# A hybrid diffusion step on one core: two groups of small products per chunk in the recurrence, and another order at the entry

## The chip, the core and the metric

The kernel runs on one core of a Trainium2 chip. The core has five engines with a queue of instructions each: TensorE (PE: matrix products into PSUM, which has eight banks per partition), VectorE (DVE), ScalarE (ACT), GpSimd (POOL) and SyncE (SP, which here only issues transfers). An engine runs its queue in order; semaphores make it wait for the others. The metric is the device time of one execution in microseconds.

## The reference

One layer of a diffusion backbone over 1024 latent and 128 context tokens of width 1024: half a SwiGLU block, a token mixer, half a SwiGLU block, a last norm. Shift, scale and gate of each norm come from a conditioning vector through a linear map. The mixer runs latent attention beside a gated linear recurrence (HGRN2), forward and backward, eight heads of 64 × 64:

```python
b = jnp.cumsum(logf.reshape(B, n, CHUNK, H, DK), axis=2)
A = jnp.einsum('bntshk,bnthk,bnshk->bnhts', decay, qc, kc)
o_intra = jnp.einsum('bnhts,bnshv->bnthv', A, vc)
dS = jnp.einsum('bnshk,bnshv->bnhkv', kc * jnp.exp(g[:, :, None] - b), vc)
def step(S, inp):
    gj, dSj = inp
    return jnp.exp(gj)[..., None] * S + dSj, S
o_inter = jnp.einsum('bnthk,bnhkv->bnthv', qc * jnp.exp(b), S_prev)
```

All is float32; the large products are made of three products of rounded parts (high × high, low × high, high × low).

## The kernel before

A builder takes the instructions as the program records them, makes every dependence into a semaphore wait, and sets each engine's order by priorities and assumed costs of its own; `keep_in_program_order` pins some of them. So the order on an engine is not always that of the code.

**Entry** (`consts`, `start`). Three small transfers (the conditioning vectors cc, the vectors vec, an identity) and then the large ones are issued on SyncE: for each of eight tiles of the model width two transfers of the conditioning weights (wada) and one of the tokens (x), with two weight tiles (raw) near the front. TensorE sums the conditioning for tile k (`sums`, L159), turns it (`vectors`, L175), ScalarE and VectorE scale and split the tokens (`split`, L532 and L533), and TensorE adds the tile's part to seven running products (`unit`, names ps, bh, bl, wh, wl). `consts` also makes the recurrence's lower bounds from two exponentials on ScalarE (L305, L306).

**Recurrence** (`hgrn`). Eight heads of three chunks of 384 tokens make 24 chunks. A chunk is worked by a pair of generators. `scan_pre` makes decayed keys and queries (Kb, Qb, KE, QP) on ScalarE, VectorE and GpSimd. `scan_lev` has steps, each ending at a `yield`:

- the first products: keys by queries inside blocks of 32, one half of the partitions per direction, into two PSUM banks (lv), from which VectorE's masked copy (COPY_PREDICATED, L1093) takes the parts within blocks of 8 into A1 and A2;
- levels 8, 16, 32 and 64: products of KE's halves (kr) by QP into one more lv bank (L1086), a copy out, and the scaling of KE and QP for the next level (L1123);
- the transposed keys (kt, L1138), and then the state products dS (L1148).

After a head's third chunk `scan_out` runs the state chain S (L1158) and the output products po (L1168, L1171). The lv tiles share three banks in turn. `group` runs such steps one after the other, so that their small products stand together on TensorE; between groups `slots` lays projection products (mm: 128 × 384, in halves of 12) that belong to other parts of the mixer. A chunk has three groups, and two chunks are in flight: the first products with level 32 of the chunk before; level 8 with that chunk's level 64 and transposes; level 16 with its dS.

Of the kernel before, what the change touches and what calls it, by code (L numbers as in the profile page):

```python
# [9 lines left out]
F32 = mybir.dt.float32  # L10
# [3 lines left out]
AF = mybir.ActivationFunctionType  # L14
# [5 lines left out]
P = 128  # L20
# [7 lines left out]
NCH = T // CW  # L28
# [5 lines left out]
H = 8  # L34
# [59 lines left out]
class Trunk:  # L94
# [27 lines left out]
    def start(self):  # L122
        nc, a, pp, fp = self.nc, self.a, self.pp, self.fp
        pin = self.tc.keep_in_program_order
# [72 lines left out]

        var = {}
# [27 lines left out]
        self.lnexp()  # L226
# [4 lines left out]
        ps = {u: self.bank(t, "ps", cols[u[1]]) for u, t in zip(units, homes)}  # L231
        vectors(0, sums(0))
        for k in range(KT):
            last = k == KT - 1
# [6 lines left out]
            if k and not last:  # L241
                row = sums(k + 1)
# [37 lines left out]
    def consts(self):  # L280
        nc, cp, a = self.nc, self.cp, self.a
        self.cc = cp.tile([P, KT, 2], F32, name="cc")
        nc.sync.dma_start(self.cc, a["cc"])
# [13 lines left out]
        self.hg = self.vec[:, 109:110]  # L297
        g0, g1 = self.vec[:, 110:118], self.vec[:, 118:126]
# [6 lines left out]
        nc.scalar.activation(e0, e0, AF.Exp)  # L305
        nc.scalar.activation(e1, e1, AF.Exp)  # L306
# [559 lines left out]
    def hgrn(self):  # L866
# [145 lines left out]
    def scan_pre(self, d, b):  # L1012
# [42 lines left out]
        nc.gpsimd.tensor_tensor(e8(qp), e8(Qb), bc(TQ, 8), ALU.mult)  # L1055
        d["pre"] = Kb, Qb, KE, Tm
        yield

    def scan_lev(self, d, b):
# [30 lines left out]
        pair = (A, lv()), (B, lv())  # L1090
# [4 lines left out]

        def key_half(m):
            kr = self.kr[m]
            nc.scalar.copy(hm(kr, m)[A, :, 0], hm(KE, m)[A, :, 0])
            nc.scalar.copy(hm(kr, m)[B, :, 1], hm(KE, m)[B, :, 1])

        key_half(8)
        yield
        for li, m in enumerate((8, 16, 32, 64)):
            ps = lv()
# [20 lines left out]
            if m < 64:  # L1125
                key_half(2 * m)
# [1341 lines left out]
```

## Time and profile before

| | |
|---|---|
| median of 3 runs | 2812.59 us (2812.43 to 2813.1) |
| profiled execution, own time | 2817.01 us |
| its span, first to last instruction | 2815.2 us |
| TensorE busy | 2755.8 us (98%) |
| VectorE busy | 2040.4 us (72%) |
| recurrence | from 866 to 1390 us of the span |
| entry, to the first main product | 11.75 us |

Times of instructions are in us from the span's start. In a row of a timeline stand start, duration, engine, line, operation, output<-inputs, shape and count, and in brackets how long the engine sat idle just before and what ended that. A row of waits gives the total, the number of times and the longest. A TensorE product has two records where its operands are plain float32. Products are pipelined, so the distance between starts tells a product's price better than its duration.

### The profile page before, as it was taken

To read this page: it belongs to the slowest core of one execution; us is meant where nothing else is said; L and a number is where in the kernel's file an instruction comes from. 1 tells how busy PE (TensorE), PEld (TensorE's weight loads), DVE (VectorE), ACT (ScalarE), POOL (GpSimd) and SP (SyncE) were. 2 spreads that over 40 slices of the span, in tenths; PEclk is the share of its full clock that TensorE was granted. 3 is DMA by queue.
4 is the path that set the end of the run, shared out by engine and by line. 5 is a ranking of instruction groups with operands and counts; after the bars stand their busy time and mean duration, and the time that the engine had idled before them with its cause. 6 is when DMAs were issued, how large, how long until landed. Compare 5 with 4: busy or idle time off the path is not lost. (4 is left out here: it accounts for less than half of the span.)

```text
span 2815.2 us, 55727 instructions
## 1 busy us (share of the span) xinstructions
PE 2755.8 (98%) x21222; PEld 2630.0 (93%) x21222; DVE 2040.4 (72%) x4461; ACT 1303.7 (46%) x2696; POOL 924.2 (33%) x983
## 2 busy tenths in 40 slices
PE   8999999999999999999999999999999999999998
PEld 7999999999999998899998778689999999999997
DVE  7877777677778888887466777767666665568875
ACT  6522323321166677666536777741642322235332
POOL 0133323454222222212234444431414343423451
PEclk9999999999999999999999999999999999999999
DMA  6743343653121111112512001263454444357521
GB/s 258 223 134 122 123 125 126 241 202 110 60 91 59 44 61 46 61 51 78 195 61 93 19 15 29 85 242 121 142 168 136 150 147 135 111 169 253 160 85 68
DMA packets 219578, 337.64 MB, mean 120 GB/s; under 512 B 23664, under 2 KB 141360, under 8 KB 219312
## 3 DMA queue, kind: packets, MB, share of 16 engines
q1 hardware_dynamic: 219312, 334.10, 36.2%
q8 instruction: 167, 2.74, 0.4%
q14 instruction: 99, 0.81, 0.1%
HBM read 248.47 MB, written 85.54 MB: 119 GB/s over the span
## 5 line engine op out<-in xcount | busy, mean ns | idle before, releaser
L1920 PE MATMUL b<-xo,wo 128*128 128x288 f32 x3552 | 483.7, 295 | 1.0 <-DVE wo L1895 1.0
L1920 PEld LDWEIGHTS b<-xo,wo 128*128 128x128 f32 x3552 | 475.4, 188 | 1.3 <-DVE wo L1895 1.3
L1920 PE MATMUL b<-bh,wo 128*128 128x288 f32 x1776 | 366.3, 295 | 0.2 <-DVE hf L1853 0.2
L539 PE MATMUL mm<-xh,wh 128*128 128x384 f32 x928 | 323.5, 349 | 4.3 <-DVE sg L851 3.1
L541 PE MATMUL mm<-xh,wl 128*128 128x384 f32 x928 | 314.0, 338 | 0.0
L540 PE MATMUL mm<-xl,wh 128*128 128x384 f32 x928 | 313.1, 337 | 0.0
L1920 PEld LDWEIGHTS b<-bh,wo 128*128 128x128 f32 x1776 | 288.8, 188 | 0.4 <-issue 0.4
L569 DVE SCALAR_TENSOR_TENSOR x<-dn,modt,x 128x256 f32<-128x256 f32 (+4 forms) x472 | 226.0, 499 | 82.6 <-PE dn L541 80.3
L1920 PE MATMUL b<-bl,wo 128*128 128x288 f32 x888 | 261.9, 295 | 0.0
L1894 ACT CAST wo<-raw 128x512 fp32r<-128x512 f32 x185 | 114.7, 621 | 221.2 <-issue 83.9
L2121 PE MATMUL d<-xd,wd 128*128 128x288 f32 x1344 | 181.7, 297 | 5.4 <-DVE x L2108 3.2
L2121 PEld LDWEIGHTS d<-xd,wd 128*128 128x128 f32 x1344 | 180.0, 190 | 7.0 <-ACT wd L2059 2.2
L539 PEld LDWEIGHTS mm<-xh,wh 128*128 128x128 f32 x928 | 174.7, 188 | 10.9 <-DVE sg L851 3.5
L1895 DVE TENSOR_TENSOR wo<-raw,wo 128x512 fp32r<-128x512 f32 x185 | 127.4, 689 | 79.1 <-ACT wo L1894 75.7
L540 PEld LDWEIGHTS mm<-xl,wh 128*128 128x128 f32 x928 | 174.9, 188 | 0.9
L541 PEld LDWEIGHTS mm<-xh,wl 128*128 128x128 f32 x928 | 174.9, 188 | 0.0
L1617 POOL TENSOR_TENSOR ehl<-e,ehl 128x512 fp32r<-128x512 f32 x93 | 123.7, 1335 | 154.7 <-ACT ehl L1615 86.1
L393 DVE SCALAR_TENSOR_TENSOR junk<-wada,cb 128x512 bf16<-128x512 f32 x224 | 165.2, 738 | 4.3 <-DMA wada<-in_w_aT 3.6
L1920 PEld LDWEIGHTS b<-bl,wo 128*128 128x128 f32 x888 | 167.4, 189 | 0.0
L1890 POOL TENSOR_TENSOR ws<-raw 128x256 f32<-128x256 f32 x74 | 65.7, 909 | 283.4 <-DMA raw<-in_w 211.2
L539 PE MATMUL ps<-bh,wh 128*128 128x288 f32 (+1 forms) x448 | 136.0, 304 | 4.1 <-ACT bh L532 1.5
L1895 DVE TENSOR_TENSOR wo<-ws,wo 128x512 fp32r<-128x512 f32 x74 | 70.2, 948 | 91.5 <-ACT wo L1894 89.9
(477 smaller groups left out, 7165.6 us busy)
## 6 DMA issues: line engine op xcount, KB each, us to landing
raw<-in_w SPq DMA_DIRECT2D x148, 256.0 KB, 3.5
wada<-in_w_aT SPq DMA_DIRECT2D x112, 256.0 KB, 3.0
raw<-in_w SPq DMA_DIRECT2D x42, 512.0 KB, 3.8
raw<-in_w_in SPq DMA_DIRECT2D x41, 512.0 KB, 3.6
xr<-xd SPq DMA_DIRECT2D x56, 288.0 KB, 3.9
hr<-hs SPq DMA_DIRECT2D x26, 576.0 KB, 5.5
hb<-hd SPq DMA_DIRECT2D x44, 288.0 KB, 3.8
hs<-et SPq DMA_DIRECT2D x84, 144.0 KB, 2.3
```

The costliest lines, as they stand in the source:

```text
L393: nc.vector.scalar_tensor_tensor(junk, ws[n % 2], 1.0, cs[s], ALU.mult, ALU.mult, accum_out=o)
L539: pin(nc.tensor.matmul(ps, wh, xh, start=start and i == 0, stop=False))
L540: pin(nc.tensor.matmul(ps, wh, xl, start=False, stop=False))
L541: self.last_mm = nc.tensor.matmul(ps, wl, xh, start=False, stop=stop and i == n - 1)
L569: nc.vector.scalar_tensor_tensor(self.x[m][:, a:b], ps[:, a - lo : b - lo], self.modt[:, gm, m, s : s + 1], self.x[m][:, a:b], ALU.mult, A ...
L1617: eng.tensor_sub(el, e, eh)
L1890: nc.gpsimd.tensor_tensor(o[:, c], x[:, c], y[:, c], op)
L1894: nc.scalar.copy(wh, src[i])
L1895: nc.vector.tensor_sub(wl, src[i], wh)
L1920: nc.tensor.matmul(ps, w[:, k], x[:, k, :QW], start=first, stop=last, skip_group_check=home != i)
L2121: nc.tensor.matmul(ps, w[:, k], xv, start=start, stop=stop, skip_group_check=home != i)
```

## The change

In the recurrence the first products and level 8 become one step: the first products of the forward half and the level-8 products get two halves of one bank (`both`), and level 8's keys are copied already at the end of `scan_pre`. A chunk then takes six steps, spread over two groups a chunk and three passes: first products and level 8 with the last chunk's level 32 and the dS of the one before that; then level 16 with the last chunk's level 64 and transposes. The slots between groups become 4 and 3 or 4 (before 3, 2 or 3, and 2), the same sum. `scan_out` comes one pass later.

At the entry the three small transfers are issued on ScalarE's queue, the bounds' exponentials come after ScalarE's second table load, and TensorE gets eight products of a tile of ones before the first conditioning sums and five after the first `vectors`.

```diff
+        def spin(n):
+            p = pp.tile([P, P], F32, tag="ps1", bufs=1, name="warm")
+            for _ in range(n):
+                pin(nc.tensor.matmul(p, self.ones, self.ones, start=True, stop=True))
...
-        self.lnexp()
+        self.bounds(self.lnexp())
...
-        vectors(0, sums(0))
+        spin(8)
+        row = sums(0)
+        vectors(0, row)
+        spin(5)
...
-        nc.sync.dma_start(self.cc, a["cc"])
+        pin = self.tc.keep_in_program_order
+        pin(nc.scalar.dma_start(self.cc, a["cc"]))
...
-        nc.sync.dma_start(self.vec, a["vecs"])
+        pin(nc.scalar.dma_start(self.vec, a["vecs"]))
...
-        nc.sync.dma_start(self.ident, a["ident"])
+        pin(nc.scalar.dma_start(self.ident, a["ident"]))
...
+    def bounds(self, table):
...
-        nc.scalar.activation(e0, e0, AF.Exp)
-        nc.scalar.activation(e1, e1, AF.Exp)
+        self.behind(nc.scalar.activation(e0, e0, AF.Exp), table)
+        self.behind(nc.scalar.activation(e1, e1, AF.Exp), table)
...
-        old = cur = out = last = None
-        for p in range(H * NCH + 1):
+        older = old = cur = out = last = None
+        for p in range(H * NCH + 2):
             h, n = divmod(p, NCH)
-            old, cur, pre = cur, None, iter(())
+            older, old, cur, pre = old, cur, None, iter(())
...
-            self.group(old, cur)
-            slots(3)
-            self.group(old, cur, old, out)
-            slots(2 + p % 2)
-            self.group(cur, out, old)
+            self.group(older, old, cur)
             out = None
-            if p and n == 0:
+            if p > 1 and n == 1:
                 out = self.scan_out(last if h < H else d)
                 next(out)
-            slots(2)
+            slots(4)
+            self.group(out, old, cur, out, old)
+            slots(3 + p % 2)
             for _ in pre:
                 pass
-        self.group(out, out)
...
+        self.key_half(KE, 8)
         d["pre"] = Kb, Qb, KE, Tm
         yield
...
-        pair = (A, lv()), (B, lv())
+        both = self.pp.tile([P, 2, 3, 64], F32, tag="lv", bufs=3, name="lv")
+        pair = (A, both[:, 0]), (B, lv())
         products(pair, Kb, Qb, diag)
         for dst, mi, (_, ps) in zip((A1, A2), (0, 1), pair):
             nc.vector.copy_predicated(dst, mb(mi), ps[:, :, :G])
...
-        key_half(8)
-        yield
         for li, m in enumerate((8, 16, 32, 64)):
-            ps = lv()
+            ps = both[:, 1] if m == 8 else lv()
```

The order in which the built programs' instructions stand, at three places.

TensorE, one chunk before: level 32 of the chunk before (kr_9108) and the first products (Qb, Kb), then projection products (36 in all, of which two rows are shown).

```order
L541 MATMUL mm<-xh_8538,wl 128x384
L1086 MATMUL lv<-QP,kr_9108 32x32 x12
L1086 MATMUL lv<-Qb,Kb 32x32 x24
L539 MATMUL mm<-xh_8524,wh 128x384
L540 MATMUL mm<-xl_8525,wh 128x384
```

The same chunk now (kr_9123 is level 32, kr_9121 level 8):

```order
L1156 MATMUL dS<-V,kT 64x64 x6
L1101 MATMUL lv<-QP,kr_9123 32x32 x12
L1101 MATMUL lv<-Qb,Kb 32x32 x24
L551 MATMUL mm<-xh_8539,wh 128x384
L552 MATMUL mm<-xl_8540,wh 128x384
L553 MATMUL mm<-xh_8539,wl 128x384
L1101 MATMUL lv<-QP,kr_9121 32x32 x12
L551 MATMUL mm<-xh_8541,wh 128x384
```

Level 8 stands three projection products behind the first products; before, it stood in the next group.

VectorE now, ahead of a masked copy out of the first products' banks (L1109, which was L1093): two weight subtractions, then state updates (S) around the level-32 scaling of QP.

```order
L1132 TENSOR_TENSOR Gall<-T_10983 128x3
L358 TENSOR_TENSOR wl<-raw,wh 128x512 x2
L1166 SCALAR_TENSOR_TENSOR S<-S,Gall,dS 64x64
L1131 TENSOR_TENSOR QP<-QP,T_10272 64x6x32
L1166 SCALAR_TENSOR_TENSOR S<-S,Gall,dS 64x64
L1132 TENSOR_TENSOR T_11157<-T_11032 128x12
L1166 SCALAR_TENSOR_TENSOR S<-S,Gall,dS 64x64
L1109 COPY_PREDICATED A_1_9128<-mask,lv 128x96
L1109 COPY_PREDICATED A_9129<-mask,lv 128x96
L1050 TENSOR_TENSOR Kb<-kk,X 64x384
```

Three state updates now stand around and ahead of the copies; the first of them waits for the dS that heads the same group on TensorE.

ScalarE at the entry, the change's rows with + and those before with −:

```order
-L305 ACT_TABLE_LOAD
-L305 ACTIVATE lbe_77<-lbe_77 128x8
-L306 ACTIVATE lbe_78<-lbe_78 128x8
+L2463 UNCONDITIONAL_BRANCH
+L292 DMA cc<-in_cc 128x16
+L294 DMA vec<-in_vecs 128x126
+L296 DMA ident<-in_ident 128x128
 L127 ACT_TABLE_LOAD
 L127 ACTIVATE sc<-cc 128x8x2
-L433 ACT_TABLE_LOAD
+L445 ACT_TABLE_LOAD
+L317 ACTIVATE lbe_122<-lbe_122 128x8
```

The three transfers stand ahead of everything on ScalarE, one table load is gone, and the exponentials follow the conditioning's activation.

More of the change, by code (lines that the diff above doesn't have):

```diff
@@ L297, in consts @@
         self.hg = self.vec[:, 109:110]
+    def bounds(self, table):
+        nc, cp = self.nc, self.cp
         g0, g1 = self.vec[:, 110:118], self.vec[:, 118:126]
@@ L1055, in scan_pre, with key_half @@
         nc.gpsimd.tensor_tensor(e8(qp), e8(Qb), bc(TQ, 8), ALU.mult)
+        self.key_half(KE, 8)
         d["pre"] = Kb, Qb, KE, Tm
         yield
+    def key_half(self, KE, m):
+        kr, src = [t.rearrange("p (n h m) -> p n h m", h=2, m=m) for t in (self.kr[m], KE)]
+        for r, side in ((slice(0, 64), 0), (slice(64, P), 1)):
+            self.nc.scalar.copy(kr[r, :, side], src[r, :, side])
     def scan_lev(self, d, b):
@@ L1125, in scan_lev @@
             if m < 64:
-                key_half(2 * m)
+                self.key_half(KE, 2 * m)
             if m < G:
```

4 lines of the change are left out of this document (removed).

## The prediction

> **What bounds the kernel now.** I read the page's busy times first, then the busy time by stretch, then who TensorE waits for in the recurrence, then the timeline around the small products.
>
> ```profile
> PE 2755.8 (98%) x21222; PEld 2630.0 (93%) x21222; DVE 2040.4 (72%) x4461; ACT 1303.7 (46%) x2696; POOL 924.2 (33%) x983
> 866.00:1390.00 524.00, 512.25 (x6127) 478.91 (x6127) 404.83 (x1040) 348.27 (x861) 125.39 (x204) 1.00 0.22 72
> ```
>
> TensorE is busy 98% of the span. A time changes only where TensorE idles, runs its products slowly or switches kinds of product. The recurrence (866 to 1390, the second row: length, then busy time of TensorE, its weight loads, VectorE, ScalarE and GpSimd) has 524 − 512.25 = 11.75 us of TensorE idle time in all; nothing in it can win more than this plus the cost of switching. VectorE is the busiest engine behind it: 404.83/524 = 77%.
>
> ```profile
> PE lv L1086 <- DVE QP L1123: 7.0, 6, 1.8
> PE mm L539 <- DVE sg L851: 3.1, 2, 1.6
> PE lv L1086 <- DVE A L1093: 0.7, 1, 0.7
> ```
>
> All but 1 us of that idle time is TensorE waiting for VectorE. The third row matters most: once, the level-8 products waited for the masked copy (L1093) that reads the chunk's first products (Qb, Kb) out of their PSUM bank.
>
> **The small products and their edges.** TensorE around one chunk's first products:
>
> ```profile
> 1003.11 0.33 PE L540 MATMUL mm<-xl,wh 128*128 128x384 f32 x1
> 1003.28 0.34 PE L541 MATMUL mm<-xh,wl 128*128 128x384 f32 x1
> 1003.55 0.40 PE L1086 MATMUL lv<-QP,kr 128*32 128x32 f32 x24
> 1003.88 0.62 PE L1086 MATMUL lv<-Qb,Kb 64*32 64x32 f32 x48
> 1004.43 0.44 PE L539 MATMUL mm<-xh,wh 128*128 128x384 f32 x1
> 1004.71 0.34 PE L540 MATMUL mm<-xl,wh 128*128 128x384 f32 x1
> 1004.88 0.33 PE L541 MATMUL mm<-xh,wl 128*128 128x384 f32 x1
> ```
>
> Starts of projection products are 0.17 us apart. Into a group it is 0.27 (1003.28 to 1003.55), out of it 0.28 (1004.43 to 1004.71). A group's two edges therefore cost 0.10 + 0.11, about 0.2 us. With 24 chunks, one group fewer in each would win 24 × 0.2 = 4.8 us.
>
> The built order shows that this mostly doesn't happen. In 19 of 24 chunks the level-8 products do not stand in the group of the first products: one to four projection products lie between them, three in most. I count five groups fewer in all: **−1.0 us**.
>
> **The wait that is added.** The level-8 products now write the bank (both[:, 1]) whose other half (both[:, 0]) the masked copy reads, and the program makes their first one wait for that copy, in all 24 chunks. Before, the same wait existed through the turn of the three banks, but 24 or 36 projection products lay in front of it, over 4 to 6 us. Now the cover is three of them. The three chunks where VectorE is latest, the one where it is early, and the first and the last of the 24:
>
> ```profile
> 866.27 0.62 PE L1086 MATMUL lv<-Qb,Kb 64*32 64x32 f32 x48
> 870.23 0.21 DVE L1093 COPY_PREDICATED A<-mask,lv 128x96 f32<-128x96 uint8 x1
> 1046.48 0.62 PE L1086 MATMUL lv<-Qb,Kb 64*32 64x32 f32 x48
> 1052.23 0.42 DVE L1093 COPY_PREDICATED A<-mask,lv 128x96 f32<-128x96 uint8 x2
> 1176.67 0.62 PE L1086 MATMUL lv<-Qb,Kb 64*32 64x32 f32 x48
> 1184.10 0.42 DVE L1093 COPY_PREDICATED A<-mask,lv 128x96 f32<-128x96 uint8 x2
> 1184.51 0.89 PE L1086 MATMUL lv<-QP,kr 128*64 128x64 f32 x36 [0.71 <-DVE A L1093]
> 1281.55 0.62 PE L1086 MATMUL lv<-Qb,Kb 64*32 64x32 f32 x48
> 1282.57 0.42 DVE L1093 COPY_PREDICATED A<-mask,lv 128x96 f32<-128x96 uint8 x2
> 1301.80 0.62 PE L1086 MATMUL lv<-Qb,Kb 64*32 64x32 f32 x48
> 1307.71 0.41 DVE L1093 COPY_PREDICATED A<-mask,lv 128x96 f32<-128x96 uint8 x2
> 1345.85 0.62 PE L1086 MATMUL lv<-Qb,Kb 64*32 64x32 f32 x48
> 1346.88 0.41 DVE L1093 COPY_PREDICATED A<-mask,lv 128x96 f32<-128x96 uint8 x2
> ```
>
> Call d the time from the first products' start to the copy's start. TensorE goes on 0.41 us after the copy's start (1184.10 to 1184.51). Without a wait, level 8 would start 1.27 us after the first products: 0.55 to the next projection product, 0.28 + 0.17 + 0.17 to the third one's end, 0.10 to switch. The stall of a chunk is d + 0.41 − 1.27 = d − 0.86.
>
> - Lower bound: the least d is 1.02, so 24 × 0.16 = 4 us.
> - Upper bound: the 24 d add up to 72.5 us (pairs like those shown), so 72.5 − 24 × 0.86 = 52 us, if VectorE stays as late as it is.
> - What I take. VectorE runs its queue in order; d is long where more is queued ahead of the copy than the gap holds. In the chunk whose VectorE order the part on the change shows, six scalings, two weight subtractions, three state updates and seven short instructions now lie between the level-64 scaling and the copy. By the rows below that is 6 × 0.40 + 2 × 0.74 + 3 × 0.32 + about 2 = 6.9 us, against 36 projection products and the small ones, 36 × 0.17 + 2 = 8.2 us. The same sum over the other chunks leaves slack in 21 of 24, mostly 2 us or more. So the backlog there goes, and d is near its least, plus the one or two state updates or key scalings that the new order puts right before the copy:
>
> ```profile
> L1158 DVE SCALAR_TENSOR_TENSOR S<-S,Gall,dS 64x64 f32<-64x64 f32 x112 | 35.9, 321 | 12.0 <-ACT dS L1149 9.1
> L1123 DVE TENSOR_TENSOR KE<-KE,T 64x192 f32<-64x192 f32 x184 | 72.7, 395 | 7.6 <-ACT kr L1099 2.1 <-ACT kr L1098 2.0
> L346 DVE TENSOR_TENSOR wl<-raw,wh 128x512 fp32r<-128x512 f32 x70 | 50.0, 742 | 16.7 <-ACT wh L342 14.1 <-DMA wrec<-wl 1.9 <-ACT sg L739 0.3
> ```
>
> About 0.3 us more: 21 × (0.16 + 0.3) = 9.7 us. The other three are those at 1046, 1176 and 1301. There the norm of a finished head pair (L444 to L446) or gates (L851) are queued as well; the same sum gives 21 to 22 us of VectorE work from copy to copy against 17 to 20 us of TensorE, after as before. I keep their d: 5.75 + 7.43 + 5.91 − 3 × 0.86 = 16.5 us. Together **+26 us**. Behind the waiting product stand 44 to 47 projection products in TensorE's queue, so the whole stall is seen.
>
> The page "PSUM — Partial Sum Buffer" of the Trainium skill, section "PSUM bank collisions raise a hardware error", says that a product's write and VectorE's read must be kept apart by bank and not by address. By it this wait is no caution of the builder that a disjoint half would spare; if it were one, the 26 us would be 0. The row at 1184.51 shows the wait as real.
>
> **What is won in exchange.** Between groups lie 36 to 48 projection products instead of 24 to 36, and each stall at level 8 lets VectorE catch up. The 7.0 us of waits for QP should go: **−7 us** (bounds 0 and −8, the first and third rows of waits together). The dS products of the third chunk in flight have a whole gap more for their transposed keys, which cost nothing before either. The level-8 key copies, 2 per chunk on ScalarE, move ahead of the chunk; ScalarE is busy 348 of 524 us and takes them there. At the end of the recurrence only 12 projection products, not 24, lie between the last dS and the output products: 0 to 2 us, I take **+0.5**.
>
> **Entry.** Issues, the first products and their pitch:
>
> ```profile
> 0.74 0.38 SPq L283 DMA_DIRECT2D cc<-in_cc  x1
> 2.11 0.91 SPq L148 DMA_DIRECT2D wada<-in_w_a  x2
> 11.75 0.61 PE L539 MATMUL ps<-bh,wh 128*128 128x288 f32 x1 [1.49 <-ACT bh L532]
> 13.88 0.44 PE L539 MATMUL ps<-bh,wh 128*128 128x288 f32 x1
> 14.12 0.44 PE L540 MATMUL ps<-bl,wh 128*128 128x288 f32 x1
> 14.25 1.05 ACT L353 CAST wh<-raw 128x1024 fp32r<-128x1024 f32 x1 [1.70 <-DMA raw<-in_w]
> 16.18 1.94 PE L159 MATMUL adap<-wada,sc 128*32 128x128 f32 x32
> 19.27 0.29 PE L541 MATMUL ps<-bh,wl 128*128 128x288 f32 x1
> 19.40 0.30 PE L539 MATMUL ps<-bh,wh 128*128 128x290 f32 x1
> 19.89 1.08 PE L159 MATMUL adap<-wada,sc 128*32 128x128 f32 x32
> 1026.94 2.20 PE L1182 MATMUL ops<-osq,onesb 128*128 128x384 f32 x6
> 1028.69 0.63 PE L539 MATMUL mm<-xh,wh 128*128 128x384 f32 x1
> ```
>
> The first large transfer issues at 0.74 instead of 2.11: 1.37 us earlier, and with it all that waits for it. The first 12 products run 0.24 us apart (13.88 to 14.12), later ones 0.13 (19.27 to 19.40); the sums take 1.94, later 1.08. With TensorE kept busy from 1.2 us on, this slow time would go: about 11 × 0.11 + 0.86 = 2.1 us. A product of ones is a third of an ops product, (1028.69 − 1026.94)/9 = 0.19 us, at the slow pitch 0.36: eight are 2.9 us, inside the idle time before the first sums at 6.16; five are 1 to 1.8 us in the 1.5 us that TensorE waits before 11.75, so they may delay it by 0.3. But the second weight tile is waited for at 14.25, and it comes only 1.4 us earlier; the products that need it follow with some 2 us to spare. Of 3.5 us I take **−3** (bounds −1 and −3.6).
>
> The page "DMA: Bandwidth & Descriptors" of the Trainium skill, section "Issuing engines are not separate DMA queues", says that a second issuing queue adds no bandwidth, it only spares issue time. By that alone this edit gives its 1.37 us; no row here prices more.
>
> **Sum**, against the profiled execution's 2817.01 us (span 2815.2): +26 + 0.5 − 7 − 1 − 3 = +15.5. That execution lies 4.4 us above the median of 2812.59, so the time is 2812.6 + 15.5 = **2828 us**.
>
> **The rivals.**
> 1. *Faster: the cover is enough.* If VectorE reaches the copy within 0.86 us of the first products, it costs nothing; the point of decision is d below about 1.3 in nearly all chunks, the three late ones too. Then 4 − 7 − 1 − 3 = −7: 2806. For it: the slack in 21 chunks. Against it: three chunks whose queue hasn't changed.
> 2. *No change.* The late chunks stall half as much and the others 0.2: 8 + 4 − 11 = +1: 2814.
> 3. *Much slower: VectorE stays as late as now.* +52 − 1 − 3, and the waits for QP stay: 2860. For it: the d of 2.7 to 4.5 in seven other chunks. Against it: their queue ahead of the copy is shorter now.
> 4. *The change does what its words say*: the builder's place is of no account, 24 edges go and no wait is seen: −4.8 − 7 − 3 = −15: 2798. Against it: the order.
>
> **How the numbers follow.** Forecast 0.55, rival 1 0.12, rival 2 0.16, rival 3 0.14, rival 4 0.03. A measurement here can't tell less than 0.2%, 5.6 us, from no change: faster is below 2807, slower above 2818.2. Rivals 1 and 4 are faster (0.15); rival 2 and a little of the forecast's low end are the same (0.18); the rest is slower (0.67). The forecast's own range, with late chunks at half and ordinary ones at 1 us, is 2819 to 2840. The range for 8 in 10 takes in rival 1 and most of the way to rival 3: 2805 to 2850.
>
> **What would show it.** Right: TensorE's list of waits gets a row of level-8 products waiting for VectorE's masked copy, about 24 times, 15 to 35 us, the longest 4 to 7 us and near the two roots; the row for QP all but goes; the first projection product runs at 0.13 us pitch and some 3 us earlier. Wrong: that row is under 8 us, or the stall turns up at another instruction (the state updates waiting for ScalarE, say), or the early products still run at 0.24.

## The result, and the profile after

The changed kernel takes 2845.82 us (median; 2843.55 to 2848.77), the kernel before 2812.85 us beside it: ratio 1.0115, 95% interval 1.0103 to 1.0127. The change costs 33 us. The forecast was 2828 us, a loss of 15.5: the sign is right, the size is less than half of what was measured.

The profiled execution of the changed kernel took 2845.94 us, with a span of 2844.1: 28.9 us more than the span before (2815.2). The other 4 us lie in the reference: the profiled execution before stood 4.4 us above its median; what held it up is not shown.

The busy times of the page after, and the recurrence from its first products to its last norm sums (length, then busy time of TensorE, weight loads, VectorE, ScalarE, GpSimd, then the granted clock):

```profile
PE 2768.1 (97%) x21248; PEld 2644.4 (93%) x21248; DVE 2050.6 (72%) x4461; ACT 1304.4 (46%) x2695; POOL 928.4 (33%) x983
867.76:1421.79 554.03, 518.86 (x6130) 486.67 (x6129) 413.30 (x1038) 350.48 (x856) 126.03 (x203) 0.98 0.21 71
```

The same stretch before, in one row:

```profile
866.27:1389.09 522.82, 511.07 (x6123) 478.31 (x6123) 404.83 (x1040) 347.14 (x860) 124.48 (x204) 1.00 0.22 72
```

So the recurrence grew by 31.2 us. TensorE's idle time there grew from 11.75 to 35.2 us, and the granted clock fell from 1.00 to 0.98. Whom TensorE waits for there, after (total, times, longest):

```profile
PE lv L1101 <- DVE A L1109: 30.8, 22, 5.8
PE po L1179 <- DVE S L1166: 3.5, 1, 3.5
...
```

The first row is the added wait: level-8 products (L1101) behind VectorE's masked copy (L1109). The row for the scaled queries (7.0 us before) is gone. The second row is new: the last output products wait for the last states.

TensorE at the longest stall, in order of time. The row at 1187.90 is the first products, the one at 1195.56 level 8:

```profile
1187.90 0.62 PE L1101 MATMUL lv<-Qb,Kb 64*32 64x32 f32 x48
...
1189.25 0.34 PE L552 MATMUL mm<-xl,wh 128*128 128x384 f32 x1
1189.42 0.34 PE L553 MATMUL mm<-xh,wl 128*128 128x384 f32 x1
1195.56 0.55 PE L1101 MATMUL lv<-QP,kr 128*32 128x32 f32 x24 [5.80 <-DVE A L1109]
1196.05 0.69 PE L551 MATMUL mm<-xh,wh 128*128 128x384 f32 x1
1196.53 0.52 PE L552 MATMUL mm<-xl,wh 128*128 128x384 f32 x1
1196.85 0.52 PE L553 MATMUL mm<-xh,wl 128*128 128x384 f32 x1
...
1201.01 0.43 PE L551 MATMUL mm<-xh,wh 128*128 128x384 f32 x1
1201.28 0.34 PE L552 MATMUL mm<-xl,wh 128*128 128x384 f32 x1
1201.46 0.34 PE L553 MATMUL mm<-xh,wl 128*128 128x384 f32 x1
```

Read the starts behind the stall. From 1196.53 to 1201.01 fourteen projection products start 0.32 us apart; before the stall and from 1201.28 on the distance is 0.17 to 0.18. The stall costs 5.80 us, and the products behind it 14 × 0.145 = 2.0 us more. Nothing is waited for in these 4.5 us. The granted clock shows why, in a window of 20 us around the stall and in the stretch of it that is slow (the clock is the third number from the right):

```profile
1180.00:1200.00 20.00, 13.76 (x188) 12.88 (x187) 18.20 (x45) 12.62 (x33) 8.40 (x12) 0.77 0.24 78
1190.96:1201.20 10.24, 5.64 (x40) 5.58 (x41) 9.21 (x27) 5.15 (x14) 2.32 (x4) 0.50 0.33 104
```

In all, 57 projection products of this execution run 0.32 us apart, against 10 before: 47 × 0.145 = 6.8 us. Ten of the 57 stand just ahead of the recurrence, from 863.3 to 866.5. They follow a wait that the profile before doesn't have, for a gate that stands on ScalarE behind a key copy (kr):

```profile
861.81 0.44 PE L551 MATMUL mm<-xh,wh 128*128 128x384 f32 x1 [2.10 <-ACT sg L751]
861.02 0.35 ACT L1072 COPY kr<-KE 64x192 f32<-64x192 f32 x1 [5.27 <-DVE KE L1131]
```

This wait and the slow products behind it, 2.1 + 1.5 us, are why the recurrence starts 1.5 us later than before (867.76 against 866.27), though the entry had won 2.75 us.

Waits and slow products together explain most of the recurrence itself. Without its idle time and slow products it took 522.8 − 11.75 − 1.5 = 509.6 us before. After, with the other 47 slow products, it took 554.0 − 35.2 − 6.8 = 512.0 us, with six more projection products inside it (6 × 0.175 = 1.0 us). The small products of the slow stretches are not counted; 1.4 us stay unexplained.

The entry, after:

```profile
1.05 3.78 PE L201 MATMUL warm<-ones 128*128 128x128 f32 x16 [1.05 <-DVE ones L298]
6.42 1.93 PE L159 MATMUL adap<-wada,sc 128*32 128x128 f32 x32 [1.59 <-ACT sc L127]
9.88 2.48 PE L201 MATMUL warm<-ones 128*128 128x128 f32 x10 [0.53 <-DVE modt L179]
12.01 0.59 PE L551 MATMUL ps<-bh,wh 128*128 128x288 f32 x1
...
13.56 0.29 PE L551 MATMUL ps<-bh,wh 128*128 128x288 f32 x1
13.68 0.29 PE L552 MATMUL ps<-bl,wh 128*128 128x288 f32 x1
...
17.14 1.08 PE L159 MATMUL adap<-wada,sc 128*32 128x128 f32 x32
```

The first main product starts 0.26 us later than before (12.01 against 11.75), but the pitch is at 0.13 from 13.5 on, not from 19, and the third sums come 2.75 us earlier (17.14 against 19.89).

### The profile page after: what moved, and what is told of

It is laid out like the page before. It is cut to its first block, busy times and chain, and to the rows that moved or that the text cites. A ratio compares the mean times of both kernels' runs of the same rounds, so it can differ in the third digit from the quotient of the medians.

```text
span 2844.1 us, 55719 instructions
## 1 busy us (share of the span) xinstructions
PE 2768.1 (97%) x21248; PEld 2644.4 (93%) x21248; DVE 2050.6 (72%) x4461; ACT 1304.4 (46%) x2695; POOL 928.4 (33%) x983
## 3 DMA queue, kind: packets, MB, share of 16 engines
q8 instruction: 168, 2.75, 0.4%
## 5 line engine op out<-in xcount | busy, mean ns | idle before, releaser
L1131 POOL TENSOR_TENSOR QP<-QP,T 64x192 f32<-64x192 f32 x96 | 54.6, 577 | 252.8 <-PE lv L1101 243.9
## 6 DMA issues: line engine op xcount, KB each, us to landing
raw<-in_w SPq DMA_DIRECT2D x42, 512.0 KB, 4.0
raw<-in_w_in SPq DMA_DIRECT2D x41, 512.0 KB, 3.5
```

The lines of the kernel that those rows point to most:

```text
L1131: eng.tensor_tensor(v, v, bc(tt[r], m), ALU.mult)
```

## The experiments

Two theories stood at the start. **Theory 1**: the loss is the level-8 wait at the shared bank, the slow clock behind its long stalls, and the late states at the end. **Its rival**: two groups and a third chunk are themselves too much for VectorE, and the bank shows it first. Ratios are to the kernel before, timed beside it on the same chip (medians 2813.7 to 2814.6 us there); compare ratios, not times. "Waits" are TensorE's in the recurrence, between 863 and 1425 us.

### The two halves of the change

The entry alone in the kernel before, and the recurrence alone:

```diff
-        nc.sync.dma_start(self.cc, a["cc"])
+        pin(nc.scalar.dma_start(self.cc, a["cc"]))
...
+        spin(8)
+        row = sums(0)
+        vectors(0, row)
+        spin(5)
```

> The kernel before, with the entry's part of the change alone (the three small transfers on ScalarE's queue, the thirteen products of ones, the bounds behind the table load); the recurrence is as before. Theory 1 (the loss of 33 us comes from the recurrence alone): the third sums of the modulation come 2.75 us earlier in the changed kernel (17.14 against 19.89) and nothing behind them takes it back, so 2812.9 - 2.75 = 2810 us (2808 to 2812), and the recurrence's first products start near 866.27 - 2.75 = 863.5. Rival (the entry gives its gain back before the recurrence, since in the changed kernel the recurrence starts at 867.76, 1.5 us later than before): 2813 to 2816 us, and the first products at 866 or later.

Ratio 0.9990 (0.9981 to 0.9999), −2.8 us; the recurrence starts at 863.80 instead of 866.27. As theory 1 had it: without the recurrence's change the entry's gain is kept.

> The changed kernel with the entry as before: only the recurrence's part of the change. Theory 1 (level-8 wait, slow clock after long stalls, late states at the end, all in the recurrence): the changed kernel's 2845.8 us plus the entry's gain of 2.75: 2848.5 us (2846.5 to 2850.5); the level-8 products wait 28 to 33 us in all for the masked copy. Rival (the entry's part costs something, a start of the recurrence 1.5 us later): 2842 to 2845 us.

Ratio 1.0111 (1.0098 to 1.0125). The time, 2845.48 us, lies between the two ranges. The level-8 wait is 32.1 us, 52 products are slow. The entry's 0.1% is less than these two intervals can tell apart, so this run decides nothing on the entry; it shows that the loss is the recurrence's. The wait for a gate just ahead of the recurrence is here too (2.11 us, at 861.07), with the old entry, while the entry alone has none: it belongs to the recurrence's change.

### A bank of its own for level 8

```diff
-        both = self.pp.tile([P, 2, 3, 64], F32, tag="lv", bufs=3, name="lv")
-        pair = (A, both[:, 0]), (B, lv())
+        pair = (A, lv()), (B, lv())
...
-            ps = both[:, 1] if m == 8 else lv()
+            ps = lv()
...
-        for tag, n in (("lv", 3), ("mm", 2), ("sm", 3)):
+        for tag, n in (("lv", 4), ("mm", 2), ("sm", 2)):
```

> The changed kernel, but the level-8 products write a bank of their own: four banks for the level products instead of three, two for the small ones (transposes, state increments, output products, norms) instead of three. Everything else of the change stays: two groups a chunk, three chunks in flight. Theory 1 (the shared bank is the cause): the row of waits for the masked copy (30.8 us) falls below 3 us, the granted clock in the recurrence is 1.00 but for one or two stretches (about 9 us of slow products less), the waits for QP stay away; the two small banks may cost 0 to 6 us. So 2845.8 - 30 - 9 + 3 = 2810 us (2804 to 2816). Rival (two groups a chunk and a third chunk in flight are themselves too much for VectorE, the bank only shows it first): VectorE is as late as before, another product waits in place of level 8, 2825 to 2845 us, with 15 us or more of TensorE waiting for VectorE in the recurrence.

Ratio 1.0046 (1.0034 to 1.0059). The shared bank is worth 0.69%, 19 us, over half of the loss, and this is net of what two small banks instead of three cost. But the time doesn't come down to the kernel before. Its waits:

```profile
PE mm L551 <- DVE sg L863: 8.2, 3, 3.4
PE mm L551 <- ACT sg L751: 4.8, 3, 3.0
PE kt L1145 <- ACT oT L1181: 3.5, 3, 2.1
PE ops L1189 <- DVE rt L456: 2.9, 3, 1.3
PE po L1178 <- DVE S L1165: 2.7, 2, 1.9
PE mm L551 <- DVE q L779: 2.4, 1, 2.4
...
```

The copy's row is gone, and 25.5 us of other waits stand in its place. At the three late places TensorE now runs into the projection banks (mm), which VectorE and ScalarE have not read yet: 3.25 us at 1055, 2.97 at 1192, 3.43 at 1318. So the rival holds for the part that is left, and **theory 2** was formed: with two groups the work falls due in lumps, and TensorE meets a lump wherever it next needs VectorE or ScalarE.

### The clock behind the stalls

```diff
         products(pair, Kb, Qb, diag)
+        fill = {10: 22, 11: 9, 16: 28, 22: 24}.get(self.cnt, 0)
+        if fill:
+            warm = self.pp.tile([P, P], F32, tag="sm", bufs=3, name="warm")
+            for _ in range(fill):
+                nc.tensor.matmul(warm, self.ones, self.ones, start=True, stop=True)
```

> The changed kernel with 22, 9, 28 and 24 products of ones put in front of the level-8 products of the four chunks with the longest stalls (4.67, 2.12, 5.80 and 4.87 us; a product of ones is about 0.19 us, so they take 4.2, 1.7, 5.3 and 4.6 us). Nobody uses their result. VectorE sets when level 8 may start, so the stall itself is not shortened: TensorE only isn't idle in it. Theory 1 (idle time of 2 us and more lowers TensorE's clock for the products behind it): the 41 projection products that ran at a pitch of 0.32 instead of 0.175 behind these four stalls run at 0.175, 41 x 0.145 = 6 us, with the small products some 7: 2839 us (2836 to 2841), and the granted clock is 1.00 in those stretches. Rival (the clock falls there for another reason, or the waiting alone is the loss): 2845 to 2848 us, granted clock as in the changed kernel (0.74 near 1200, 0.91 near 1060).

TensorE around the longest stall:

```profile
1190.32 0.62 PE L1101 MATMUL lv<-Qb,Kb 64*32 64x32 f32 x48
1190.87 6.52 PE L1112 MATMUL warm<-ones 128*128 128x128 f32 x56
1198.02 0.40 PE L1101 MATMUL lv<-QP,kr 128*32 128x32 f32 x24 [0.62 <-DVE A L1114]
...
1198.62 0.34 PE L552 MATMUL mm<-xl,wh 128*128 128x384 f32 x1
1198.79 0.34 PE L553 MATMUL mm<-xh,wl 128*128 128x384 f32 x1
```

Level 8 starts 7.70 us after the first products, as in the changed kernel (7.66). The products behind it stand 0.17 us apart at once. From level 8 to the next chunk's first products it now takes 19.47 us (1198.02 to 1217.49) instead of 21.44 (1195.56 to 1217.00): the 2.0 us worked out above. None of the four filled stalls is followed by slow products: that the idle time causes them is shown here. In sum it gave less than expected: ratio 1.0104 (1.0090 to 1.0118), 2844.07 us, between the two ranges. 24 products still run slowly, eight of them behind a stall of 1.39 us at 1106 that was 0.72 us in the changed kernel. The 3 us of gain lie inside the intervals.

### Three groups, or level 8 elsewhere

```diff
-            slots(4)
+            slots(3)
+            self.group(cur)
+            slots(2 + p % 2)
             self.group(out, old, cur, out, old)
-            slots(3 + p % 2)
+            slots(2)
```

Level 8 is a step of its own here, with a bank of its own out of the turn of three.

> The changed kernel with the level-8 products as a step of their own again: a third group per chunk, 24 to 36 projection products behind the first products, in the turn of three banks. Three chunks in flight and the new entry stay. Theory 2 (formed after the run with a bank of its own for level 8, where 27.6 us of waits stayed: with two groups VectorE and ScalarE get their work in lumps, and TensorE meets the lump wherever it next needs one of them; the shared bank only makes it meet the lump at once): with three groups the waits in the recurrence are those of the kernel before (12 us) or up to 7 less, and with the entry's 2.5 us the ratio to the kernel before is 0.996 to 1.000 (2802 to 2813 us). Rival (the third chunk in flight keeps VectorE late, however many groups): 20 us or more of waits in the recurrence, ratio 1.003 or more.

Ratio 1.0051 (1.0038 to 1.0064): waits of 21.3 us, 42 slow products. Theory 2 was wrong here, or the placing of the levels was; the run with the third chunk alone, below, decides.

```diff
-            self.group(older, old, cur)
+            self.group(old, older, cur)
```

Here level 8 is in the turn of the three level banks, and there are three small banks.

> The changed kernel, level 8 in a bank of its own, but out of the turn of the three level banks (the small ones keep three): level 8 then takes the bank of the older chunk's level 32, which therefore goes first in the group and is read by ScalarE. Two groups, three chunks, new entry. Theory 2 (lumps): in the run with two small banks 17.5 us of the waits were for the projection banks (gates and q, read by VectorE and ScalarE) and 7.4 us for small banks. The 7.4 go, the 17.5 stay, level 8 waits 0.2 to 0.4 us a chunk for ScalarE (5 to 10 us): ratio 1.002 to 1.006 (2819 to 2830 us). Rival (the two small banks were what cost there, the projection banks only in their train): below 10 us of waits in the recurrence, ratio 0.995 to 0.999.

Ratio 1.0065 (1.0052 to 1.0078), just above theory 2's range. The row `PE kt` of the small banks is gone, the projection banks' waits stay (10.1 us for gates), and level 8 pays more for its bank than expected:

```profile
PE lv L1101 <- ACT Af L1119: 10.9, 18, 3.2
PE mm L551 <- DVE sg L863: 8.6, 2, 4.4
PE lv L1101 <- DVE A L1108: 6.1, 1, 6.1
```

```diff
+            src = ps[:, :, :G]
+            if mi == 0:
+                src = tmp("Ax", 2, (P, 3, G))
+                nc.scalar.copy(src, ps[:, :, :G])
-            nc.vector.copy_predicated(dst, mb(mi), ps[:, :, :G])
+            nc.vector.copy_predicated(dst, mb(mi), src)
```

> The changed kernel, but ScalarE copies the first half's products out of the shared bank to SBUF, and VectorE's masked copy reads them there. So level 8 waits for ScalarE (busy 356 of 560 us in the recurrence) and not for VectorE (418 of 560). One more ScalarE instruction a chunk. Theory 1 (the place of the wait is what counts): 21 stalls of about 0.8 us fall to 0.5 or less, and the three of 4.7 to 5.8 us to below 1: 2845.8 - 21 x 0.4 - 12 - 6 (slow clock) = 2820 us. Theory 2 (lumps): the stalls at level 8 go as well, but at the three late places TensorE then waits about 3 us each for a projection bank, as with a bank of its own: 2825 to 2833 us. Rival (ScalarE is queued as deep as VectorE): 2840 us or more, level 8 waiting 25 us or more for ScalarE.

Ratio 1.0074 (1.0062 to 1.0087), 2833.69 us, just above theory 2's range. Another reader takes 13 of the 30.8 us of the wait away, where theory 2 had these stalls gone; the gates' waits appear as it says:

```profile
PE lv L1101 <- ACT Ax L1112: 17.8, 23, 3.5
PE mm L551 <- DVE sg L863: 5.0, 3, 2.0
```

### The end of the recurrence

```diff
-            slots(4)
+            slots(4 if h < H else 2)
```

> The changed kernel, except that in the last two turns of the recurrence two projection slots, not four, are taken between the groups, so that 24 projection products stand between the last state increments and the output products, not 12. Theory 1: the wait of the output products for the last states (3.5 us) falls to 1.4 or less (12 x 0.175 = 2.1 us more cover) and the slow clock behind it (5 products, 0.7 us) goes: 2845.8 - 2.8 = 2843 us. Rival (the states come as late as before because the level-64 and key work ahead of them is squeezed by the shorter cover): the wait moves to the transposed keys or the increments, 2845 to 2847 us.

Ratio 1.0093 (1.0077 to 1.0108). The wait of 3.5 us for the last states is gone from the list and no other took its place. The ratio falls by 0.22%, 6 us; the trace accounts for 3.5 + 0.7 of them, and the intervals overlap.

### VectorE's load

```diff
-                (B, nc.vector, qp, 0, tR),
+                (B, nc.gpsimd, qp, 0, tR),
```

This edit was made in the changed kernel, in the kernel before with the new entry, and in the kernel with a bank of its own and the cover at the end:

> The changed kernel with one of VectorE's three scalings per level (the lower half's queries) moved to GpSimd, which does the upper half's already: 96 x 0.46 = 44 us off VectorE's 413 in the recurrence, 96 x 0.57 = 55 us more for GpSimd's 126 of 552. Theory 2 (VectorE's own load is the bound at the late places: 27 to 28 us busy in 30 there): some 1.8 us less per chunk; the backlog of the three late places is worked off over about two chunks, so their stalls fall by 2 to 4 us each and the others by up to 0.4, 30.8 us of waits for the masked copy to 12 to 20, and the slow clock behind them with it: 2845.8 - 14 - 4 = 2828 us (2822 to 2834). Rival (GpSimd's scalings come too late): the next level's products wait for GpSimd, 10 us or more, and the time stays at 2840 us or above.

Ratio 1.0108 (1.0094 to 1.0122): nothing, and theory 2 missed. The wait for the copy is still 29.6 us, the longest 4.5 instead of 5.8. VectorE's busy time in the recurrence fell from 413.3 to 396.8 us, not by the 44 us expected, so a VectorE with much less to do was not tried. What holds the copy back is read from the rows: what stands ahead of it in VectorE's queue. VectorE during the longest stall of the changed kernel:

```profile
1188.37 0.54 DVE L863 TENSOR_TENSOR sg<-mm,sg 128x384 f32<-128x384 f32 x1
1189.01 0.98 DVE L1042 TENSOR_TENSOR X<-fs,X 128x48 f32<-128x48 f32 x1
1190.02 0.93 DVE L1058 TENSOR_TENSOR TQ<-Y,fs 64x48 f32<-64x48 f32 x1
...
1191.47 1.05 DVE L1043 RECIPROCAL Y<-X 128x144 f32<-128x144 f32 x1
1192.44 1.22 DVE L358 TENSOR_TENSOR wl<-raw,wh 128x512 fp32r<-128x512 f32 x2
...
1195.25 0.42 DVE L1109 COPY_PREDICATED A<-mask,lv 128x96 f32<-128x96 uint8 x2
```

A gate, the next chunk's preparation and two weight subtractions come first, and of scalings one only (0.36 us, at 1194.70). In the longest stall of the run with the scaling on GpSimd none stands there (1187.51 to 1192.01).

> The kernel before with the new entry and the same scaling moved to GpSimd; recurrence in the order of before. Theory 2: the waits for the scaled queries (6 us) and for the gates (3 us) shrink by half or more: ratio 0.996 to 0.9985 (2802 to 2809 us), below the 0.999 of the entry alone. Rival (GpSimd is the later one): the level products wait for GpSimd's scaling instead, ratio 1.000 or more.

Ratio 0.9975 (0.9966 to 0.9985), 2806.3 us: faster than both kernels, as theory 2 expected. Its waits in the recurrence are 5.7 us in all, against 12.1 before; the longest row:

```profile
PE lv L1098 <- POOL QP L1135: 3.3, 2, 3.0
...
```

> Level 8 in a bank of its own (ratio 1.0046 alone), the same scaling on GpSimd, and 24 instead of 12 projection products before the output products at the end. Theory 2: of the 24.9 us of waits there for projection and small banks about half go with VectorE's 44 us, 2.7 us at the end too: 2827 - 12 - 3 = 2812 us, ratio 0.998 to 1.002. Rival (two groups leave the lumps as they are, whatever VectorE's total): 20 us or more of waits stay, ratio 1.003 or more.

Ratio 1.0005 (0.9997 to 1.0014), 17.6 us of waits. In the range of theory 2, but 8 us dearer than the same scaling in the old order.

### The third chunk alone

```diff
-            self.group(old, cur)
+            self.group(older, old, cur)
+            out = None
+            if p > 1 and n == 1:
+                out = self.scan_out(last if h < H else d)
+                next(out)
             slots(3)
             self.group(old, cur, old, out)
             slots(2 + p % 2)
-            self.group(cur, out, old)
-            out = None
-            if p and n == 0:
-                out = self.scan_out(last if h < H else d)
-                next(out)
+            self.group(cur, out)
             slots(2)
```

> The kernel before in its three groups (level 32 with the first products; level 64, level 8 and the keys; level 16), with the new entry, and of the recurrence's change only the third chunk: the state increments go into the first group of the next turn, and the state updates and output products follow one group later. In the run with three groups the levels stood otherwise (8 alone, 64 together with 16), so that run does not tell the third chunk from the place of the levels. Theory 2 (lumps: what counts is how much of VectorE's work falls due in one group): the waits stay at those of the kernel before (12 us) or fall a little, ratio 0.997 to 1.0005 (2805 to 2815 us). Rival (the third chunk itself makes VectorE late, since state updates then meet the norm and the gates): 20 us or more of waits in the recurrence, ratio 1.003 or more.

Ratio 1.0039 (1.0025 to 1.0052), against 0.9990 for the entry alone: the third chunk by itself costs some 14 us (the level-8 key copies at the end of `scan_pre` are in this kernel too). The rival is right. Its main rows (the first about as long as before the change, the second longer, the third new):

```profile
PE lv L1103 <- DVE QP L1133: 6.8, 4, 2.7
PE mm L551 <- DVE sg L863: 5.8, 2, 3.0
PE po L1181 <- DVE S L1168: 4.7, 1, 4.7
...
```

**Theory 3**: it is not the chunk in flight but what it delays. The state updates need the last chunk's increments, and with a turn's delay they come a group later.

```diff
-            out = None
-            if p > 1 and n == 1:
-                out = self.scan_out(last if h < H else d)
-                next(out)
...
-            self.group(cur, out)
+            self.group(cur, out, old if n == 0 else None)
+            out = None
+            if p and n == 0:
+                out = self.scan_out(last if h < H else d)
+                next(out)
...
+        self.group(out, out)
```

> The run with the third chunk alone (ratio 1.0039, and 1.0049 against the new entry alone), but only two of three chunks have their state increments in the next turn: the last chunk of a head keeps them in the third group of its own turn, as before the change, so that the state updates on VectorE and the output products stand where they stood. Theory 3 (the third chunk costs because the fourteen state updates of a head, 14 x 0.33 = 4.7 us of VectorE, come a group later, into the stretch in which the norm of the pair and the gates are queued, and at the end too late for the output products): ratio 0.998 to 1.000 (2808 to 2814 us), the waits for gates and queries back at about 9 us, no wait for the last states. Rival (any chunk more in flight costs, by the increments and the key copies of level 8 that go ahead): ratio 1.002 or more, waits for gates and queries of 12 us or more.

Ratio 1.0002 (0.9993 to 1.0011). Some 10 of the 14 us are back, with two of three chunks still a turn longer in flight. What went, by the list of waits: the states (4.7), 1.8 of the queries, the 1.6 for ScalarE's gates, 0.9 for the norm.

```profile
PE mm L551 <- DVE sg L863: 5.6, 2, 2.8
PE lv L1104 <- DVE QP L1134: 5.0, 4, 2.7
```

The two long waits for gates stay at 2.8 us, so the part of theory 3 that sends the state updates into the norm's and the gates' stretch is not borne out; the late states are. The 0.1% that this kernel stands above the entry alone is within the intervals.

> The kernel of early states with one scaling per level on GpSimd as well, beside the best so far (order before the change, new entry, that scaling on GpSimd: ratio 0.9975). Theory 3: no dearer than that one, since two of three increments merely stand a group later: ratio 0.9965 to 0.9985. Rival (the increments a group later cost by themselves): ratio 0.9995 or more.

Ratio 0.9977 (0.9967 to 0.9987): the same as without the third chunk (0.9975). Increments a group later are free, and bring nothing.

> The run with two groups and level 8 in a bank of its own (ratio 1.0046), with the last chunk's state increments in a small group of their own, 24 projection products after its keys, and the state updates right behind, as before the change: a third group once per head, two groups otherwise. Theory 3: the three late places lose the state updates from their queue, the waits of 3 us there fall to 1.5 or less and the small ones with them: 2827 - 10 = 2817 us, ratio 0.999 to 1.002; at the end a wait of 2 to 4 us for the states stays, since 12 projection products stand there. Rival (two groups gather VectorE's work whatever the states do): ratio 1.0035 or more, 3 us of wait at each of the three late places as before.

```profile
PE mm L551 <- ACT sg L751: 6.6, 4, 2.4
PE po L1183 <- DVE S L1170: 4.7, 1, 4.7
PE kt L1150 <- ACT oT L1186: 4.1, 2, 3.3
PE ops L1194 <- DVE rt L456: 4.0, 3, 1.3
```

Ratio 1.0045 (1.0033 to 1.0058), as with late states (1.0046). With two groups, early states win nothing. The prices of two groups, of the shared bank and of late states do not add up: each wait that goes gives way to another. Of this kernel's waits, 4.1 + 4.0 + 1.0 us are for small banks, of which it has two; whether two groups would pay with more banks can't be tried, since all eight are given out.

### All kernels in two terms

Difference of the waits from 12.1 us, 0.145 us for each slow product over ten, and −2.8 where the entry is new; beside it the difference of the spans. Slow products are projection products 0.27 to 0.36 us apart, at least three in a row, each counted in one profiled execution.

| kernel | waits | slow products | two terms | span | ratio |
|---|---|---|---|---|---|
| before | 12.1 | 10 | 0 | 0 | 1 |
| changed | 35.1 | 57 | +27.0 | +28.9 | 1.0115 |
| entry alone | 11.2 | 10 | −3.7 | −4.3 | 0.9990 |
| recurrence alone | 35.6 | 52 | +29.6 | +28.3 | 1.0111 |
| own bank | 25.5 | 26 | +12.9 | +8.3 | 1.0046 |
| ScalarE copies out | 26.7 | 31 | +14.8 | +17.2 | 1.0074 |
| three groups | 21.3 | 42 | +11.0 | +12.8 | 1.0051 |
| cover at the end | 32.9 | 64 | +25.8 | +22.8 | 1.0093 |
| turn of three | 28.8 | 48 | +19.4 | +14.9 | 1.0065 |
| third chunk alone | 20.9 | 3 | +5.0 | +7.5 | 1.0039 |
| scaling on GpSimd, changed | 32.5 | 55 | +24.1 | +23.1 | 1.0108 |
| scaling on GpSimd, order before | 5.7 | 10 | −9.2 | −10.7 | 0.9975 |
| own bank, GpSimd, end | 17.6 | 14 | +3.3 | −0.2 | 1.0005 |
| early states | 11.5 | 27 | −0.9 | −1.7 | 1.0002 |
| two groups, early states | 24.4 | 29 | +12.3 | +13.5 | 1.0045 |
| early states, GpSimd | 6.2 | 7 | −9.1 | −7.3 | 0.9977 |

No row is off by more than 5 us. The column of waits begins at 863 us. In the nine kernels of this table with two groups a wait of 2.1 us for a gate lies just ahead of that, in those with three it does not; with it the changed kernel comes to +29.1, and own bank and turn of three are off by 6.7 and 6.6. (The kernel with filled stalls is left out: its products of ones stand in idle time.) The groups' edges, of which these kernels have 55 to 77, leave no mark in this table.

## The prediction, step by step

**The shared bank, +26 us: right in kind, 4 us short.** The wait stands where it was put, 22 times, 30.8 us, where 0.7 stood before. The three late chunks were predicted at 4.9, 6.6 and 5.1 us and measured 4.67, 5.80 and 4.87. The ordinary ones were taken at 0.46 us; the 19 that show a wait have 15.4 us, 0.81 each. The copy's place behind other work in VectorE's queue was sized too small, and the slack that the sum of VectorE's work left did not bring the copy forward: by the rows of the longest stall, the order in the queue decides.

**The step that failed: the price of a stall.** The sum counted a stall as its own length. A long one also slows the products behind it: 6.8 us in the changed kernel, for which the sum has no term, and the largest of its errors. Term by term the two profiles give: level 8 +30.1 us for +26, the end +3.5 for +0.5, the other waits −10.6 (11.4 before, 0.8 after) for −7, the entry −2.8 for −3, slow products +6.8 and the wait ahead of the recurrence +2.1 for nothing. That is +29.1, and the span grew by 28.9; the other 4 us of the measured 33 are the reference's. The profile before had the sign of it, ten products 0.32 us apart from 1312.67 to 1315.55 behind a wait of 1.62 us for a gate, and a granted clock of 0.91 around them; the prediction did not use it.

**The wait ahead of the recurrence has no term.** There a key copy holds a gate back on ScalarE, because the scaling of KE that it reads comes on VectorE at 860.64, against 857.71 with the entry alone. The kernels with three groups have no such wait, the third chunk or not. Why VectorE is late there was not tried.

**The end, +0.5 us with a bound of 2: 3.5 us**, and five slow products behind it. Twelve projection products instead of 24 are 2.1 us less cover, and the state chain came later than the bound allowed for. More cover took the wait away.

**The waits for the queries, −7 us: right for the changed kernel**, but the reason holds for one half only. With the third chunk alone they are 6.8 us as ever, and with a bank of its own, where nothing waits at level 8, they stay away too; it is the 36 to 48 projection products between two groups that end them.

**The dS products of the third chunk "cost nothing": half right.** The increments themselves are free a group later, but the last chunk's carry the state updates with them. In three groups this costs 10 us (1.0039 against 1.0002). This price was not in the sum at all. In the changed kernel it is the 3.5 us at the end; more of it can't be told there, since with two groups early states changed nothing.

**Edges, −1 us:** too small to show. **The entry, −3 us:** right, 2.75 us in place and 2.8 by the times of the entry alone; in the changed kernel the wait ahead of the recurrence takes it back.

**What was to show it.** The row of level-8 products within 15 to 35 us, its longest wait of 4 to 7, the vanished row of the queries and the pitch of the early products came as named. Not named was the clock.

**The rivals.** The much slower one (2860 us) named a VectorE that stays late; late it stayed in the three chunks only. The measured time lies halfway between it and the forecast, and inside the range. The page "PSUM — Partial Sum Buffer" of the Trainium skill, section "PSUM bank collisions raise a hardware error", was cited against the thought that a disjoint half of a bank is free. The run with a bank of its own shows what the wait at this one sharing costs, 19 us; that the wait could not be left out no run here shows. By the page "DMA: Bandwidth & Descriptors" of the Trainium skill, section "Issuing engines are not separate DMA queues", the entry would have won its 1.37 us of issue time alone; it won twice that. How the gain divides between the queue and the products of ones was not tried.

## What to carry to other kernels

Price a stall of TensorE, where it is otherwise never idle, as its length plus what its clock may lose behind it, and look for that loss in the profile before: products at the wide pitch with no wait in their rows. When a wait is put on a copy, read what stands ahead of that copy in its engine's queue, instruction by instruction; the same relief of VectorE was worth nothing in one order and 0.15% in another. When a step is delayed by a turn, follow what depends on the last of its kind: the increments were free, the state updates behind the last one were not.

## What was not expected of the hardware

**A short idle time can slow TensorE.** Of the stalls over 4 us at level 8, all in the changed kernel are followed by slow products (4.67, 5.80 and 4.87 us; 7, 14 and 14 products). Of the shorter ones some are: 1.39 us (eight products, with filled stalls), 1.62 us (ten, before), 2.12 us (seven, changed), while 1.60 us in the changed kernel at 970 and 3.25 us in the kernel with a bank of its own at 1055 were followed by none. In the changed kernel the granted clock is 0.50 from 1057.84 to 1061.25, from 1327.50 to 1334.32 and from 1190.96 to 1201.20: 3.41, 6.82 and 10.24 us, each begun while TensorE was still idle. The page "TensorE: Matmul & The Clock Gate" of the Trainium skill, section "What's actually happening", says that the array falls to half clock after an idle window of about 3.4 us that runs freely. The clock of 0.50 agrees, and so do the lengths of one, two and three times 3.41 us; the pitch does roughly (0.32 against 0.175, a factor of 1.8). A fall behind 1.4 to 2.1 us of idle time, or 1.2 us into the longest stall (idle from 1189.76), comes sooner than that rule has it. What decides for a short stall stays open.

**VectorE's small instructions stretch while GpSimd works.** In the VectorE rows of the long stall above, a product of 64x48 numbers took 0.93 us, where the same line takes 0.25 us at other times (1190.02, against 1052.98 in the same kernel); GpSimd at that time:

```profile
1188.88 1.01 POOL L853 TENSOR_TENSOR sg<-sg,ohi 128x384 fp32r<-128x384 f32 x1 [3.48 <-ACT ohi L851]
1189.85 1.01 POOL L847 TENSOR_TENSOR sg<-oT,sg 128x384 f32<-128x384 f32 x1
```

The VectorE product ends at 1190.95, just after GpSimd's at 1190.86, and the one ahead of it ends at 1189.99, just after 1189.89. It looks as if the one waits for the other's end. The page "SBUF — State Buffer" of the Trainium skill, section "SBUF: two separate sides", says that a VectorE instruction with two SBUF inputs and a GpSimd instruction that reads SBUF take a shared port in turn, each for its whole length; these rows agree. It also bears on the scaling moved to GpSimd: VectorE lost 96 products of 0.42 us, 39 us, but its busy time in the recurrence fell by 29 only (405.7 to 376.4, against the entry alone), and the other scalings went from a mean of 397 ns to 431.

**A small transfer on a queue of its own can land later.** The 8 KB of cc landed 1.8 us after issue on SyncE's queue before, and 4.1 us on ScalarE's queue after, where it runs beside the large transfers that are issued at the same moment (0.73 us). The table load behind it starts at 4.85 instead of 4.30 us. The entry gains all the same.
